# The weights' subtractions issued apart from their casts, and the next queries' split behind the softmax

## The chip, the cores and the metric

The kernel runs on one core of one Trainium2 chip. The metric is the device time of one execution in microseconds (us); the median of several runs is compared. The engines are TensorE (PE in the profile; its weight loads are PEld), VectorE (DVE), ScalarE (ACT), GpSimd (POOL) and SyncE (SP, which here issues the loads of the weights). Each engine works through its own queue in order; an instruction whose operands are not there yet holds up all that stand behind it.

## What is computed

The program is a model of two blocks on 512 rows of 1024 features, all in float32. The first block has two layers of token mixing (a pool branch, sparse attention over the best keys of an index, attention to a memory) followed by 16 experts of which each row uses two. The second block is a gated feed-forward stage, a mixer (a gated delta recurrence beside dilated band attention) and a second feed-forward stage. Cut to the parts that the change touches:

```python
def attend_block(args):                    # sparse attention, per 128 queries
    ...
    s = jnp.einsum('bqhd,bqkhd->bqhk', qb, kg) * (ATT_HEAD_DIM ** -0.5)
    p = jax.nn.softmax(jnp.where(valid[:, :, None, :], s, -jnp.inf), axis=-1)
    return jnp.einsum('bqhk,bqkhd->bqhd', p, vg)

def run_block(args):                       # one expert
    h = jax.nn.silu(xb @ w1[e]) * (xb @ w3[e])
    return h @ w2[e]

def second_block(x, ...):
    x = x + 0.5 * swiglu(rms_norm(x, ffn1_norm), ...)
    proj = rms_norm(x, mix_norm) @ w_in
    o_a = gdn_mixer(...)                   # recurrence
    o_b = dilated_mixer(...)               # band attention
    x = x + jnp.concatenate([o_a, o_b], axis=-1) @ w_out
    ...
```

## The kernel before

**Split products.** PE multiplies in a reduced float32 form. To keep float32 accuracy, both operands are split into a high half (a cast on ACT) and a low half (the original less the cast, on DVE), and each product is made of three: high by high, low by high, high by low. Names end in H and L: xTH, xTL are activations, wH, wL are weights, gH/gL and hH/hL the gathered rows and the hidden rows of an expert, qs the queries of an attention (one tile holds both halves).

**The stream of weights.** `Stream` cuts all weights into 708 units of up to 128 x 1024 and handles them in the order of use: `load` issues a transfer on SP into a staging buffer (wR, or one that is lent: wX, wY, wZ, X), `split` casts (line 182, wH<-wR) and subtracts (line 185, wL<-wR,wH) and then calls `load` for the next unit, since the staging buffer is free. 13 units are marked slow; their subtraction goes to POOL. `split` is called by `tick`, at most once in 1000 ns of the planner's time, as long as a place for the halves is free, or by `need`, when a product asks for a unit that has not been split. `Panel.H` and `Panel.L` hand the halves to the products.

**The planner.** The program is written out by a Python planner that keeps a clock of its own, `now`: each product adds an estimate of its time (`adv`, which also calls `tick`), and side tasks (attention, pooling, the recurrence) are generators that yield how long they want to wait. So the order of each engine's queue is fixed when the program is built.

**The attentions.** `paired` hands out scores for two heads at a time: `pair` makes both on PE (line 810, into two buffers sa), `scores` returns them one after the other. Before the second head's scores are returned, the next pair's queries are split (`halves`, which calls `split` of lines 355 and 356: a cast on ACT and a subtraction on DVE, 128 x 128). `attention` runs three stages over the heads: `first` takes the scores and makes the softmax (line 926 adds the mask and reduces on DVE, 928 is the exponential on ACT, 929 and 930 the reciprocal and the scaling on DVE), `second` transposes P on PE (line 890) and copies it out on ACT (892, PT), `third` multiplies with V (lines 294 and 303). Sparse attention (`dsa`) and band attention (`band_attention`) both use them.

**Other names in the rows.** pd/pdL and brL are splits of the pool branch; th are the products of an expert's hidden rows (lines 1352, 1353); cu is the convolution of the recurrence (1923), Gc its summed gates (2028), go and cs its output; mg and sig the gates that merge the branches.

Of the kernel before, what the change touches and what calls it, by code (L numbers as in the profile page):

```python
# [83 lines left out]
class Panel:  # L84
    def __init__(self, ws, key, units, n):
        self.ws, self.key, self.units, self.n = ws, key, units, n
        self.k = [(u, j) for u in units for j in range(u.kc)]
# [7 lines left out]
    def L(self, k):  # L95
        u, j = self.k[k]
        if u.L is None:
            self.ws.need(u)
        return u.L[:, j * u.n:(j + 1) * u.n]


class XT:


    def __init__(self, H, L):
        self.H, self.L, self.want = H, L, {}
# [15 lines left out]
class Stream:  # L122


    def __init__(self, kern, pool, nr, nh):
        self.kern, self.pool, self.nr, self.nh = kern, pool, nr, nh
        self.places = list(range(nh))
        self.units, self.panels = [], []
        self.issued = self.split_n = self.used = self.got = 0
        self.after, self.pace = 0.0, 1000  # L130
        self.base, self.lent = 0, []
        self.limit = 1 << 30

    def plan(self, key, w, kc, n, slow=False):
        per = max(1, 1024 // n)
        units = []
        k = 0
        while k < kc:
            m = min(per, kc - k)
            src = w[k * 128:(k + m) * 128, :].rearrange("(k p) n -> p k n", p=128)  # L140
            units.append(Unit(src, m, n))
            units[-1].slow = slow
            k += m
        self.units += units
        self.panels.append(Panel(self, key, units, n))
# [27 lines left out]
    def split(self):  # L173

        if self.split_n >= self.issued or self.split_n - self.used >= self.nh:
            return False
        nc = self.kern.nc
        u = self.units[self.split_n]
        n = u.kc * u.n
        u.H, u.L = self.turn([128, 1024], F32R, "w")  # L180
        eng = nc.vector
        nc.scalar.copy(u.H[:, :n], u.R[:, :n])  # L182
        if u.slow:
            eng = nc.gpsimd
        eng.tensor_tensor(u.L[:, :n], u.R[:, :n], u.H[:, :n].bitcast(F32), OP.subtract)  # L185
        self.split_n += 1
        if u.place is None:
            self.base -= 1
        else:
            self.lent.append(u.place)  # L190
        self.load()
        return True

    def turn(self, shape, dtype, name):

# [14 lines left out]

    def tick(self):

        if self.kern.now >= self.after and self.split_n < self.limit and self.split():
            self.after = self.kern.now + self.pace

# [17 lines left out]
class Kern:  # L233
# [581 lines left out]
    def paired(self, n, q, k, *pool):  # L815

        state = []

        def split(i):
            return self.halves(q(i), *pool) if i < n else None  # L820
        nxt = [0, split(0)]

        def scores():
            if not state:
                state.extend(self.pair(nxt[1], *k(nxt[0])))
                return state[0]
            nxt[:] = [nxt[0] + 1, split(nxt[0] + 1)]
            ps = state[1]
            state.clear()
            return ps  # L830
        return scores
# [45 lines left out]
    def attention(self, pool, scores, v, add, width, out, tag="sa"):  # L877
# [3 lines left out]
        nc = self.nc  # L881

        def first(st, qb, h):
            st["P"] = self.softmax(scores(), add(qb, h), width(qb), pool)

        def second(st, qb, h):
            W = width(qb)
# [192 lines left out]
    def ending(self, l, p, r, gb, last):  # L1080
# [23 lines left out]
        begin(0)  # L1104
        begin(1)
        split()
        scale(0)
        roots(0, 1)
# [1295 lines left out]
```

## Time and profile before

| | |
|---|---|
| median of 3 runs | 3045.59 us (3044.25 to 3047.68) |
| the profiled execution: its time, its span | 3044.89 us, 3043.2 us |
| mean granted clock of PE | 0.952 |
| PE busy | 2806.0 us, 92% |
| DVE busy | 1901.8 us, 62% |
| ACT busy | 1284.3 us, 42% |
| POOL busy | 445.7 us, 15% |

The span runs in stages, in us from its start: the first layer's mixing to 560 (sparse attention in 212 to 440) and its experts to 905, the second layer likewise to 1420 and 1795, the first feed-forward stage to 2180, the panels of the recurrence and the windows to 2385, band attention with the recurrence's chain to 2610, the output projection to 2650, the second feed-forward stage to the end. The busy shares are means over these stages. "Idle before, releaser" in a row says how long the engine stood just before an instruction and what ended that.

### The profile page before, as it was taken

What the parts mean: (1) busy time and instruction counts of PE and PEld (TensorE: products, weight loads), DVE (VectorE), ACT (ScalarE), POOL (GpSimd) and SP (SyncE); (2) the same over time, 40 slices, a digit from 0 to 9 for tenths busy, and PEclk for the clock granted to TensorE, in tenths of its full rate; (3) what the DMA queues carried; (4) which work ended last, traced back from release to release, by engine and by line L of the source; (5) the groups of instructions that cost most, each with busy time, mean ns of one, the idle gap of its engine ahead of it and who ended that gap; (6) DMA issues with size and microseconds to landing.
All of it is one profiled execution on the core that took longest, in us unless ns stands there. A gap on an engine that the chain in (4) does not pass through costs nothing. (4 is left out here: it accounts for less than half of the span.)

```text
span 3043.2 us, 38735 instructions
## 1 busy us (share of the span) xinstructions
PE 2806.0 (92%) x14315; PEld 2240.3 (74%) x14315; DVE 1901.8 (62%) x3535; ACT 1284.3 (42%) x2073; POOL 445.7 (15%) x526
## 2 busy tenths in 40 slices
PE   7989889999989898988899979999999697899998
PEld 7767668876757676777667757888888586688877
DVE  5677544798986776436799974333468636544244
ACT  3533432377863433422578832222345333322122
POOL 1000011264220000111552110000132121000000
PEclk9999999999989999999899979999999789899999
DMA  6212225899963122228799914323324400223231
GB/s 197 87 56 81 65 67 177 306 356 353 350 235 107 52 70 66 77 83 300 252 353 349 344 58 166 105 71 117 103 84 119 126 13 21 70 90 116 78 104 70
DMA packets 295587, 448.27 MB, mean 147 GB/s; under 512 B 30403, under 2 KB 155987, under 8 KB 294881
## 3 DMA queue, kind: packets, MB, share of 16 engines
q1 hardware_dynamic: 274816, 382.66, 38.3%
q0 software_dynamic: 20000, 60.99, 6.3%
q8 instruction: 114, 1.87, 0.3%
q10 hardware_dynamic: 576, 2.10, 0.2%
q14 instruction: 81, 0.66, 0.1%
HBM read 423.02 MB, written 34.65 MB: 150 GB/s over the span
## 5 line engine op out<-in xcount | busy, mean ns | idle before, releaser
L185 DVE TENSOR_TENSOR wL<-wR,wH 128x1024 fp32r<-128x1024 f32 (+2 forms) x381 | 469.2, 1254 | 269.3 <-ACT wH L182 260.2
L294 PE MATMUL mm<-xTH,wH 128*128 128x512 f32 (+1 forms) x1376 | 540.1, 393 | 0.1
L294 PE MATMUL mm<-xTH,wL 128*128 128x512 f32 (+1 forms) x1376 | 531.6, 386 | 7.5 <-DVE wL L185 7.5
L294 PE MATMUL mm<-xTL,wH 128*128 128x512 f32 (+1 forms) x1376 | 529.8, 385 | 2.3 <-DVE xTL L356 2.2
L182 ACT CAST wH<-wR 128x1024 fp32r<-128x1024 f32 (+1 forms) x394 | 399.6, 1041 | 255.1 <-PE mm L294 219.2
L294 PEld LDWEIGHTS mm<-xTH,wL 128*128 128x128 f32 x1376 | 263.2, 191 | 65.6 <-DVE wL L185 15.0
L294 PEld LDWEIGHTS mm<-xTH,wH 128*128 128x128 f32 x1376 | 264.3, 192 | 60.0 <-issue 8.9
L294 PEld LDWEIGHTS mm<-xTL,wH 128*128 128x128 f32 x1376 | 264.0, 192 | 49.8 <-DVE xTL L356 3.1
L294 PE MATMUL mm<-wH,hH 128*128 128x512 f32 (+1 forms) x608 | 241.0, 396 | 0.0
L294 PE MATMUL mm<-wH,hL 128*128 128x512 f32 (+1 forms) x608 | 239.2, 393 | 0.6 <-DVE hL L356 0.6
L294 PE MATMUL mm<-wL,hH 128*128 128x512 f32 (+1 forms) x608 | 238.6, 392 | 0.0
L294 PE MATMUL mm<-wH,xTH 128*128 128x256 f32 (+3 forms) x576 | 201.9, 351 | 10.8 <-DVE rx L758 5.3
L294 PE MATMUL mm<-wH,gH 128*96 128x512 f32 x512 | 206.7, 404 | 0.0
L294 PE MATMUL mm<-wH,gL 128*96 128x512 f32 x512 | 204.3, 399 | 0.0
L294 PE MATMUL mm<-wL,gH 128*96 128x512 f32 x512 | 203.0, 396 | 0.0
L294 PE MATMUL mm<-wH,xTL 128*128 128x256 f32 (+3 forms) x576 | 189.7, 329 | 3.6 <-DVE xTL L356 3.6
L294 PE MATMUL mm<-wL,xTH 128*128 128x256 f32 (+3 forms) x576 | 188.9, 328 | 0.0
L185 DVE TENSOR_TENSOR wL<-wX,wH 128x1024 fp32r<-128x1024 f32 x142 | 169.3, 1223 | 8.1 <-ACT wH L182 7.7
L182 ACT CAST wH<-wX 128x1024 fp32r<-128x1024 f32 x142 | 145.3, 1049 | 10.4 <-PE mm L294 9.6
L1664 DVE TENSOR_TENSOR th<-th,mm 128x512 f32<-128x512 f32 x44 | 30.3, 688 | 169.0 <-PE mm L294 169.0
L294 PEld LDWEIGHTS mm<-wH,hL 128*128 128x128 f32 (+1 forms) x608 | 107.3, 177 | 34.1 <-DVE hL L356 1.4
L294 PEld LDWEIGHTS mm<-wL,hH 128*128 128x128 f32 (+1 forms) x608 | 107.6, 177 | 30.5
(541 smaller groups left out, 5219.3 us busy)
## 6 DMA issues: line engine op xcount, KB each, us to landing
wX<-in_w SPq DMA_DIRECT2D x141, 512.0 KB, 11.3
wR<-in_w_in SPq DMA_DIRECT2D x116, 512.0 KB, 3.7
wR<-in_w SPq DMA_DIRECT2D x73, 512.0 KB, 11.0
wY<-in_w SPq DMA_DIRECT2D x69, 512.0 KB, 10.7
X<-in_w SPq DMA_DIRECT2D x56, 512.0 KB, 11.2
wZ<-in_w SPq DMA_DIRECT2D x45, 512.0 KB, 10.8
wR<-in_ffn_w_gate SPq DMA_DIRECT2D x44, 512.0 KB, 3.9
wR<-in_ffn_w_up SPq DMA_DIRECT2D x44, 512.0 KB, 4.7
```

What stands on the lines that cost most here:

```text
L182: nc.scalar.copy(u.H[:, :n], u.R[:, :n])
L185: eng.tensor_tensor(u.L[:, :n], u.R[:, :n], u.H[:, :n].bitcast(F32), OP.subtract)
L294: self.nc.tensor.matmul(ps, a, b, start=start, stop=stop)
L1664: nc.vector.tensor_tensor(th, th, u, OP.mult)
```

## The change

`split` no longer subtracts. It casts the unit, remembers it as `half`, and notes the planner's time; `subtract` issues the subtraction, gives the staging buffer back and calls `load`. `subtract` is called for a half unit by the next `split`, by `tick` once 1500 ns of the planner's time have passed since the cast, by `Panel.L` when a product asks for that unit's low half, and at once for a slow unit. In the attentions, the split of the next pair's queries moves from the place before the second head's scores are returned to the place behind that head's softmax. The first split of each attention stays where it was.

```diff
--- before.py
+++ after.py
@@ -96,6 +96,8 @@
         u, j = self.k[k]
         if u.L is None:
             self.ws.need(u)
+        if u is self.ws.half:
+            self.ws.subtract()
         return u.L[:, j * u.n:(j + 1) * u.n]
 
 
@@ -130,6 +132,7 @@
         self.after, self.pace = 0.0, 1000
         self.base, self.lent = 0, []
         self.limit = 1 << 30
+        self.half = None
 
     def plan(self, key, w, kc, n, slow=False):
         per = max(1, 1024 // n)
@@ -174,22 +177,30 @@
 
         if self.split_n >= self.issued or self.split_n - self.used >= self.nh:
             return False
-        nc = self.kern.nc
-        u = self.units[self.split_n]
+        if self.half:
+            self.subtract()
+        u = self.half = self.units[self.split_n]
         n = u.kc * u.n
         u.H, u.L = self.turn([128, 1024], F32R, "w")
-        eng = nc.vector
-        nc.scalar.copy(u.H[:, :n], u.R[:, :n])
+        self.kern.nc.scalar.copy(u.H[:, :n], u.R[:, :n])
+        self.split_n += 1
+        self.begun = self.kern.now
         if u.slow:
-            eng = nc.gpsimd
+            self.subtract()
+        return True
+
+    def subtract(self):
+
+        nc = self.kern.nc
+        u, self.half = self.half, None
+        n = u.kc * u.n
+        eng = nc.gpsimd if u.slow else nc.vector
         eng.tensor_tensor(u.L[:, :n], u.R[:, :n], u.H[:, :n].bitcast(F32), OP.subtract)
-        self.split_n += 1
         if u.place is None:
             self.base -= 1
         else:
             self.lent.append(u.place)
         self.load()
-        return True
 
     def turn(self, shape, dtype, name):
 
@@ -210,6 +221,9 @@
 
     def tick(self):
 
+
+        if self.half and self.kern.now >= self.begun + 1500:
+            self.subtract()
         if self.kern.now >= self.after and self.split_n < self.limit and self.split():
             self.after = self.kern.now + self.pace
 
@@ -820,11 +834,14 @@
             return self.halves(q(i), *pool) if i < n else None
         nxt = [0, split(0)]
 
-        def scores():
+        def scores(then=False):
+            if then:
+                if not state:
+                    nxt[:] = [nxt[0] + 1, split(nxt[0] + 1)]
+                return None
             if not state:
                 state.extend(self.pair(nxt[1], *k(nxt[0])))
                 return state[0]
-            nxt[:] = [nxt[0] + 1, split(nxt[0] + 1)]
             ps = state[1]
             state.clear()
             return ps
@@ -882,6 +899,7 @@
 
         def first(st, qb, h):
             st["P"] = self.softmax(scores(), add(qb, h), width(qb), pool)
+            scores(True)
 
         def second(st, qb, h):
             W = width(qb)
```

PE's and POOL's queues keep their order. Of the 695 weight subtractions on DVE, 264 stand later by 1 to 62 other instructions, mostly 1 to 6, and none earlier. Three places on DVE follow; lines 185, 356, 926, 929, 930, 1352, 1353, 1923 and 2028 of before are lines 198, 370, 944, 947, 948, 1370, 1371, 1941 and 2046 of the changed file.

DVE in the sparse attention of the first layer, at the second softmax of a pair over 384 keys (338 us in the trace). Before:

```order
L356 TENSOR_TENSOR pdL<-pd,pdH 128x512
L185 TENSOR_TENSOR wL<-wR,wH 128x1024
L356 TENSOR_TENSOR qs<-qT_1123,qs 128x128
L926 ISA P,st<-sa,sc 128x384
L926 ISA st 128x1
L929 RECIPROCAL st<-st 128x1
L930 TENSOR_SCALAR P<-P,st 128x384
L185 TENSOR_TENSOR wL<-wR,wH 128x1024
```

After:

```order
L370 TENSOR_TENSOR pdL<-pd,pdH 128x512
L944 ISA P,st<-sa,sc 128x384
L944 ISA st 128x1
L947 RECIPROCAL st<-st 128x1
L948 TENSOR_SCALAR P<-P,st 128x384
L370 TENSOR_TENSOR qs<-qT_1123,qs 128x128
L198 TENSOR_TENSOR wL<-wR,wH 128x1024 x2
L944 ISA P,st<-sa,sc 128x384
```

The P group moved ahead of one wL and of qs; both wL now stand behind it.

DVE at the experts of the first layer, one expert (the first rows are at 759 to 767 us in the trace, the last at 774; wX, wY, wR and X are staging buffers of the stream). Before:

```order
L185 TENSOR_TENSOR wL<-wY,wH 128x1024 x2
L356 TENSOR_TENSOR gL<-tp,gH 128x384 x2
L185 TENSOR_TENSOR wL<-wY,wH 128x1024 x2
L185 TENSOR_TENSOR wL<-X,wH 128x1024
L185 TENSOR_TENSOR wL<-wR,wH 128x1024
L1352 SCALAR_TENSOR_TENSOR th<-th,mm 96x512
L1353 TENSOR_TENSOR th<-th,mm 96x512
L185 TENSOR_TENSOR wL<-wR,wH 128x1024
L185 TENSOR_TENSOR wL<-X,wH 128x1024
L185 TENSOR_TENSOR wL<-wR,wH 128x1024
L356 TENSOR_TENSOR hL<-tp,hH 128x384
```

After:

```order
L198 TENSOR_TENSOR wL<-wY,wH 128x1024
L370 TENSOR_TENSOR gL<-tp,gH 128x384 x2
L198 TENSOR_TENSOR wL<-wY,wH 128x1024 x3
L198 TENSOR_TENSOR wL<-X,wH 128x1024
L1370 SCALAR_TENSOR_TENSOR th<-th,mm 96x512
L1371 TENSOR_TENSOR th<-th,mm 96x512
L198 TENSOR_TENSOR wL<-wR,wH 128x1024
L198 TENSOR_TENSOR wL<-X,wH 128x1024
L198 TENSOR_TENSOR wL<-wR,wH 128x1024
L370 TENSOR_TENSOR hL<-tp,hH 128x384
```

One wL moved behind the two gL, another behind the two th.

DVE in the recurrence's panels, ahead of the summed gates (2220 us in the trace). Before:

```order
L185 TENSOR_TENSOR wL<-wR,wH 128x1024
L1923 SCALAR_TENSOR_TENSOR cu<-cu,cw 128x512 x2
L185 TENSOR_TENSOR wL<-wR,wH 128x1024
L2028 COPY Gc<-sa 128x16
L2030 TENSOR_TENSOR nbg<-eG,gsm 128x16
L2031 TENSOR_SCALAR hb<-gsm 128x16
```

After:

```order
L1941 SCALAR_TENSOR_TENSOR cu<-cu,cw 128x512 x2
L198 TENSOR_TENSOR wL<-wR,wH 128x1024
L2046 COPY Gc<-sa 128x16
L2048 TENSOR_TENSOR nbg<-eG,gsm 128x16
L2049 TENSOR_SCALAR hb<-gsm 128x16
L2046 COPY Gc<-sa 128x16
L2048 TENSOR_TENSOR nbg<-eG,gsm 128x16
```

The first wL moved behind two products of cu, the second from ahead of Gc to a place further back.

## Rows read from the trace of the kernel before

**Rows 1.** PE's waits over the whole span: waiting line, awaited line, us, times, longest.

```profile
PE tp L890 <- DVE P L930: 31.4, 12, 5.3
PE tp L303 <- ACT PT L892: 25.4, 7, 9.3
...
PE mm L294 <- DVE wL L185: 8.3, 19, 0.5
```

**Rows 2.** Costliest groups of the page: busy us, mean ns, then idle before, releaser.

```profile
L185 DVE TENSOR_TENSOR wL<-wR,wH 128x1024 fp32r<-128x1024 f32 (+2 forms) x381 | 469.2, 1254 | 269.3 <-ACT wH L182 260.2
```

**Rows 3.** Timeline of DVE, 330 to 346 us: start, duration, instruction, idle before.

```profile
338.85 1.23 DVE L185 TENSOR_TENSOR wL<-wR,wH 128x1024 fp32r<-128x1024 f32 x1 [0.25 <-ACT wH L182]
...
340.19 0.55 DVE L926 CUSTOM_DVE_ANT_0 P<-sa,sc 128x384 f32<-128x384 f32 x1
```

**Rows 4.** Timelines of PE at three transposes of P, both layers.

```profile
342.29 0.88 PE L890 MATMUL tp<-ident,P 128*128 128x128 f32 x3 [4.24 <-DVE P L930]
...
427.71 1.09 PE L890 MATMUL tp<-ident,P 128*128 128x128 f32 x4 [5.31 <-DVE P L930]
...
1214.71 0.87 PE L890 MATMUL tp<-ident,P 128*128 128x128 f32 x3 [4.23 <-DVE P L930]
```

**Rows 5.** Timelines of DVE and POOL, 400 to 440 us.

```profile
422.85 2.34 DVE L185 TENSOR_TENSOR wL<-wR,wH 128x1024 fp32r<-128x1024 f32 x1
...
425.31 0.68 DVE L926 CUSTOM_DVE_ANT_0 P<-sa,sc 128x512 f32<-128x512 f32 x1
...
422.84 1.26 POOL L1063 TENSOR_TENSOR mg<-mg,sig 128x512 f32<-128x512 f32 x1 [0.62 <-DVE sig L1057]
```

**Rows 6.** Stretches: busy us of PE, PEld, DVE, ACT, POOL; granted clock; DMA.

```profile
340.11:346.94 6.83, 4.65 (x15) 3.43 (x16) 3.60 (x10) 3.42 (x7) 0.00 (x0) 0.50 0.55 153
...
600.00:880.00 280.00, 277.85 (x1341) 198.17 (x1339) 260.10 (x301) 222.69 (x275) 103.24 (x82) 0.99 1.03 353
2385.00:2610.00 225.00, 174.64 (x1318) 148.25 (x1316) 128.62 (x370) 77.73 (x210) 42.77 (x50) 0.83 0.20 55
```

**Rows 7.** DVE's waits from 2385 to 2610 us.

```profile
DVE qs L356 <- ACT qs L355: 18.2, 9, 3.2
```

**Rows 8.** Timelines of DVE, ACT and PE at one pair of band attention.

```profile
2584.87 0.29 DVE L356 TENSOR_TENSOR qs<-sqT,qs 128x128 fp32r<-128x128 f32 x1 [3.24 <-ACT qs L355]
...
2586.85 0.49 DVE L930 TENSOR_SCALAR P<-P,st 128x512 f32<-128x512 f32 x1
...
2584.54 0.30 ACT L355 CAST qs<-sqT 128x128 fp32r<-128x128 f32 x1
2585.80 0.72 ACT L928 ACTIVATE P<-P,st 128x512 f32<-128x512 f32 x1 [0.97 <-DVE st L926]
...
2586.44 0.79 PE L810 MATMUL sa<-skH,qs 64*128 64x512 f32 x2
```

**Rows 9.** Timelines of DVE and POOL, 2422 to 2428 us.

```profile
2424.42 2.63 DVE L930 TENSOR_SCALAR P<-P,st 128x512 f32<-128x512 f32 x1
...
2424.69 1.06 POOL L2197 TENSOR_TENSOR T<-C,blk 128x512 f32<-128x512 f32 x1
```

**Rows 10.** Timelines of DVE and PE at the summed gates.

```profile
2222.66 1.22 DVE L185 TENSOR_TENSOR wL<-wR,wH 128x1024 fp32r<-128x1024 f32 x1
...
2224.64 0.40 PE L2037 MATMUL sa<-ident,Gc 128*32 128x128 f32 x1 [6.04 <-DVE Gc L2028]
```

**Rows 11.** Timelines of DVE and PE at one expert of the first layer.

```profile
763.67 1.02 DVE L356 TENSOR_TENSOR gL<-tp,gH 128x384 fp32r<-128x384 f32 x2
765.00 2.36 DVE L185 TENSOR_TENSOR wL<-wY,wH 128x1024 fp32r<-128x1024 f32 x2 [0.31 <-ACT wH L182]
...
768.41 1.22 DVE L185 TENSOR_TENSOR wL<-wR,wH 128x1024 fp32r<-128x1024 f32 x1
769.55 0.68 DVE L1352 SCALAR_TENSOR_TENSOR th<-th,mm 96x512 f32<-96x512 f32 x1
...
771.87 0.39 PE L294 MATMUL mm<-wL,hH 128*96 128x512 f32 x1
```

## The prediction

> **What bounds the kernel now.** I read the page first. TensorE (PE) is by far the busiest engine (the table above), so a change on VectorE (DVE) or ScalarE (ACT) gains only where PE stands and waits for them. The waits of PE over the whole span say where that is. The largest sum is the transposes of softmax rows that wait for the scaled P on DVE (31.4 us, 12 times); next come the products with V that wait for ACT's copy of the transposed P (25.4 us, 7 times). The weights' low halves wL, which the change moves most, cost PE only 8.3 us in 19 waits of at most 0.5 us [rows 1]. So the stream's subtractions are no bottleneck as such. What they do is stand in DVE's queue: 381 of the largest form take 469.2 us busy, and another 269.3 us of DVE's idle time lies in front of them, 260.2 us of it put down to the cast on ACT [rows 2]. While DVE waits for a cast, nothing behind it starts. Where a softmax that PE waits for is what stands behind, that is on the path. The same holds for the next queries' subtraction qs, which waits for its own cast.
>
> The profiled run took 3044.9 us, 1.7 us more than its span; the median of the three runs is 3045.6. I make the sum against 3044.9 and add 0.7 at the end.
>
> **Part 1, sparse attention (both layers of the first block).** The second softmax of each pair has the next queries' split in front of it. At 338 us DVE had a wL, the qs, then the score reduction into P (line 926); afterwards the P group comes first, then qs and wL (the first place of the order, above). The reduction itself needs only scores that PE has long delivered at the two places below.
>
> First place: DVE is free 0.25 us ahead of the wL at 338.85, so at 338.6, and the reduction started at 340.19 [rows 3]. Without wL and qs ahead of it, it can start 1.6 us sooner. ACT does not give that back, since its cast of qs moves behind the exponential too. PE stood 4.24 us for this P [rows 4]; what is late next is the same P, 1.6 us earlier. Second place: the wL took 2.34 us, from 422.85, and the reduction started at 425.31, 2.46 us after it could have [rows 5], out of a stall of 5.31 us [rows 4]. The qs comes just behind P now, but ahead of the next pair's scores PE still has the four transposes of that P, 1.09 us [rows 4], so the pair does not wait for it. Two smaller stalls of this kind, at 318 and 302 us, lose a wL and a qs in front of their P, but at the first the wL then stands before a split of the pool branch (brL) that PE waits for next; I count 0.9 us for both, less than the 1.23 of one wL [rows 3]. Sum 1.6 + 2.46 + 0.9 = 4.96 a layer, and layer 2 has the same stalls 871 us later, the first of them 4.23 us long [rows 4]: **9.9 us**. Bounds: 8.1 (the two large ones alone) and 11.
>
> **Part 2, the clock.** [...] Taken **4 us** (1 a dip), bounds 0 and 9.3.
>
> **Part 3, band attention (2385 to 2610 us).** PE is busy 174.64 of 225 us there [rows 6]; DVE and ACT pass work to each other. DVE waited for the cast of qs 9 times, 18.2 us together [rows 7]. At 2584.87 one sees what that cost: DVE stood 3.24 us while ACT worked off its queue, the cast ran from 2584.54, the exponential at 2585.80 only, and P's scaling at 2586.85 [rows 8]. With the reduction done ahead, in those 3.24 us, the exponential takes the cast's place at 2584.54: 1.26 us sooner. The pair's scores start at 2586.44 and need qs [rows 8]; P would be scaled from 2585.6 to 2586.1, and qs behind it ends at 2586.3. I count five such places (2399, 2417, 2501, 2563 and 2585 us): 5 x 1.26 = **6.3 us**; at the other four something else ends about as late. Bounds: 0 (the chain there runs through POOL and the recurrence too) and 9 (half of the 18.2).
>
> [...] One P of this stretch took 2.63 us for a scaling of 0.49, while POOL ran tensor operations from 2424.69 on [rows 9, 8]; the wL of 2.34 us likewise ran beside a POOL product of 1.26 us [rows 5], against 1.23 elsewhere [rows 3]. [...]
>
> **Part 4, the recurrence's panels (2180 to 2385 us).** PE stood 6.04 us for Gc until 2224.64. In front of Gc DVE had two wL; the one of 2222.66, 1.22 us long, now stands behind it [rows 10], so I take 1.2 us. A second large stall there, at 2365 us, waits for a chain that starts with a transfer of what DVE wrote before: between 0 and 1.2, and I take 0.5, since nothing shows whether that transfer or the chain decides. **1.7 us**, bounds 0 and 3.
>
> **Part 5, what may be lost: the experts.** From 600 to 880 us PE is busy 277.85 of 280 us and DVE 260.10 [rows 6], so there is nothing to gain. But subtractions now stand behind gL, hL and the products of th. I replayed one expert by hand. The wL that ran ahead of the two gL, while these waited for their cast, now runs behind them, from 764.65; the next, before at 765.00, are 0.8 us late; the one of 768.41 goes behind the two th (769.55 and after it, 0.68 us each) and ends at 771.81 instead of 769.63, while PE uses it at 771.87 [rows 11]. That holds by 0.06 us; the others hold by 0.4 us or more, and DVE has 1.2 us to spare in a period of 17.7 us (260.10 of 280 busy) to make the lag up. I take a cost of **1 us** in all, bounds 0 and 16 (1 us for each of the 16 experts of this layer; the weights of the second layer's experts are ready earlier). In the two feed-forward stages the subtraction that PE waits for stays where it is. The loads follow the subtractions by at most 2.3 us, and PE's waits name no weight load [rows 1]: nothing. In the mixers' projections as many wL stand ahead of what PE waits for as before, others in number only: nothing.
>
> Sum: 9.9 + 4 + 6.3 + 1.7 - 1 = 20.9, so 3044.9 - 20.9 = 3024.0, and with 0.7 for the median 3024.7: **3025 us**.
>
> **The rivals.** A: only the sparse attention gains. For it: the band stretch is a tangle of chains, and a wait taken away there often gives way to another that ends within a few tenths. Then 9.9 + 2 of the clock - 1 = 10.9: 3045.6 - 10.9, about 3035. B: most is given back, because the displaced qs and wL are waited for elsewhere, above all by the next pair's scores (0.1 us of margin at 2586). 1 us at each of the 15 later pairs of band attention takes 15 of the 20.9: 3045.6 - 5.9, about 3040, on the edge of no change. C, slower: the margin of 0.06 us at the experts does not hold. It decides from the point where the lag passes the use at 771.87 by more than the 1.2 us of spare time make up before the next expert; from there DVE sets the period in the first layer. At 2.2 us of lag (771.81 - 769.63) for each of 16 experts it costs 35 us: 3024.7 + 35, about 3060. Against it: in the replay the lag is made up within each period, and PE hardly waits for wL today. D: the change does not do what it says, because the planner's clock issues most subtractions at once after all. The order rules that out: 264 of the 695 subtractions on DVE stand later, mostly by 1 to 6 instructions; so D has no chance of its own.
>
> **How the numbers follow.** Chances: forecast 0.60, A 0.16, B 0.14, C 0.10. With all upper bounds, 11 + 9.3 + 9 + 3 = 32.3, the time is 3013; chains that I did not follow may add a little, so the range starts at 3009. Above, it takes in A and nearly all of B and leaves out C: 3044. About 0.2% (6 us) is what a measurement of this kernel can tell from no change, so faster means below 3039.5. The forecast lies there but for a tail of 0.02, A but for 0.02, and B with a small part, 0.03: 0.75 faster; 0.15 within; 0.10 slower.
>
> **What would show it.** In the profile after: PE's wait for P down from 31.4 to about 22 us, its stalls at 338 and 422 us at 2.6 and 2.9 us; no qs in front of the reductions any more; the half-clock stretches there shorter. The experts are right if their stretch keeps its length within 1 us and no PE wait for wL appears in it. The forecast is wrong if the pair's scores (line 810) wait for qs, or if wL becomes a wait of PE well above its 8.3 us.

## The result

The changed kernel takes 3005.25 us, the median of 4 runs (2999.22 to 3007.87), against 3044.92 us (3039.83 to 3047.68) for the kernel before in the same comparison: a ratio of 0.9873, interval 0.9862 to 0.9885. The direction was right and the size was not: 39.7 us came where the prediction's sum had 20.9, and 3005 lies below the range, which ended at 3009.

The profiled execution after took 3007.87 us, its span is 3006.2 us, 37.0 less than before, and the mean granted clock of PE is 0.960 (0.952 before). The first line of the page after (engine, busy us, share of the span, instructions):

```profile
PE 2792.3 (93%) x14315; PEld 2227.8 (74%) x14315; DVE 1885.5 (63%) x3535; ACT 1283.9 (43%) x2073; POOL 447.3 (15%) x526
```

PE issues the same 14315 products in the same order in both kernels, so that each product of the one has its partner in the other. PE's busy time fell from 2806.0 to 2792.3, so 13.7 of the 37.0 us are the same products done faster. The granted clock is enough for them, by an estimate: of PE's busy time, 203.3 us lay in stretches at half clock before and 170.9 after. In the trace of before, products of 128 x 512 start 0.43 us apart at half clock (345.37 to 346.23 us) and 0.23 us apart at the full one (from 347.02 on), so about half of that difference, 16.2 us, is what the clock took. The other 23.3 us are idle time of PE. This split is one of the time and not of its causes: slower products can fill a wait that was idle otherwise, as in the middle of the band, where PE was busy 9.4 us less at a clock of 1.00 than at 0.83 and 3.6 of these became idle time (experiment 8). One profiled run below, that of experiment 9, took 3044.26 us, where the other four of its kernel took 2999 to 3007, and lost 38 us at the start of band attention; only its stages ahead of that are read. Between the same pairs of products, by stage (starts in the trace of before; "half clock" is the time in which the granted clock was 0.50; both traces show this value and 1.00 and no other):

| stage, us of before | length before, after | change | of it idle | of it busy | half clock before, after |
|---|---|---|---|---|---|
| mixers' projections, 120 and 1001 | 176.5, 180.1 | +3.6 | +3.0 | +0.6 | 13.7, 13.7 |
| first queries, 212 and 1085 | 177.9, 173.1 | -4.8 | -1.7 | -3.1 | 6.8, 0 |
| sparse attention, 302 to 440 | 138.0, 130.1 | -7.9 | -5.0 | -3.0 | 23.9, 13.7 |
| sparse attention, 1173 to 1310 | 137.2, 127.8 | -9.5 | -5.7 | -3.8 | 28.1, 15.1 |
| panels, 2181 to 2385 | 203.9, 197.2 | -6.7 | -4.6 | -2.1 | 23.9, 13.7 |
| band attention, 2385 to 2650 | 265.2, 258.6 | -6.6 | -6.4 | -0.2 | 81.9, 81.9 |
| all else | | -5.1 | -3.0 | -2.1 | |

Windows of the kernel after over the four lower stages say the same (busy us of PE, PEld, DVE, ACT, POOL, then PE's granted clock, DMA share, GB/s):

```profile
302.00:432.10 130.10, 117.50 (x611) 89.18 (x610) 67.37 (x165) 55.41 (x113) 12.02 (x8) 0.95 0.24 69
1162.40:1290.10 127.70, 115.84 (x591) 87.76 (x589) 67.25 (x163) 53.69 (x110) 12.03 (x8) 0.94 0.24 70
2157.30:2354.50 197.20, 178.79 (x1186) 163.67 (x1188) 144.51 (x327) 89.21 (x159) 47.27 (x152) 0.97 0.39 107
2354.50:2613.10 258.60, 213.30 (x1483) 180.72 (x1480) 139.22 (x393) 85.60 (x219) 46.26 (x51) 0.84 0.20 58
```

and those of before over the same work:

```profile
302.10:440.10 138.00, 120.45 (x611) 91.41 (x610) 71.40 (x164) 55.63 (x112) 12.16 (x8) 0.91 0.22 65
1173.10:1310.30 137.20, 119.67 (x592) 90.51 (x590) 71.26 (x163) 54.36 (x109) 12.15 (x8) 0.90 0.22 66
2181.20:2385.00 203.80, 180.80 (x1186) 165.28 (x1188) 143.64 (x326) 88.80 (x159) 49.90 (x152) 0.94 0.36 101
```

PE's waits over the span of the kernel after (waiting line, awaited line, us, times, longest), which answer [rows 1]:

```profile
PE tp L908 <- DVE P L948: 22.0, 12, 2.7
PE tp L317 <- ACT PT L910: 21.7, 7, 8.0
...
PE tp L979 <- DVE kL L800: 10.9, 2, 5.4
...
PE mm L308 <- DVE wL L198: 8.8, 20, 0.5
```

The wait for P went from 31.4 to 22.0 us, as forecast, and wL stayed where it was (8.3, 8.8). New is the length of the third line's wait: kL cost 7.9 us, 4.4 at most, before. DVE's own largest group of subtractions, which answers [rows 2], stands 170.9 us idle ahead of itself instead of 269.3:

```profile
L198 DVE TENSOR_TENSOR wL<-wR,wH 128x1024 fp32r<-128x1024 f32 (+2 forms) x381 | 463.6, 1236 | 170.9 <-ACT wH L185 169.9
```

**The two large stalls of sparse attention.** DVE and PE of the kernel after at the first (timeline: start, duration, instruction, idle before), to hold against [rows 3, 4]:

```profile
334.53 0.69 DVE L370 TENSOR_TENSOR pdL<-pd,pdH 128x512 fp32r<-128x512 f32 x1 [0.74 <-ACT pdH L369]
335.14 0.55 DVE L944 CUSTOM_DVE_ANT_0 P<-sa,sc 128x384 f32<-128x384 f32 x1
336.67 0.42 DVE L948 TENSOR_SCALAR P<-P,st 128x384 f32<-128x384 f32 x1
337.00 0.29 DVE L370 TENSOR_TENSOR qs<-qT,qs 128x128 fp32r<-128x128 f32 x1
337.21 2.35 DVE L198 TENSOR_TENSOR wL<-wR,wH 128x1024 fp32r<-128x1024 f32 x2
```

```profile
337.24 0.52 PE L908 MATMUL tp<-ident,P 128*128 128x128 f32 x3 [2.53 <-DVE P L948]
...
418.99 1.09 PE L908 MATMUL tp<-ident,P 128*128 128x128 f32 x4 [2.69 <-DVE P L948]
```

The reduction into P follows the pool branch's pdL at once; qs and two wL come behind the scaling. The stalls are 2.53 and 2.69 us; 2.6 and 2.9 were forecast. The two lines on PE also differ in what no forecast had: three transposes in 0.52 us are at the full clock (1.00 from 337.24 to 341.00 us; they took 0.88 in [rows 4]), four in 1.09 at half (0.66 in the mean from 418.99 to 428.00), as before.

**Band attention.** DVE's wait for the cast of qs, 18.2 us in 9 times before [rows 7], is one of 7.4 us, in the wait list of DVE from 2354 to 2580 us; that one stands ahead of the first pair, whose split the change leaves in its place:

```profile
DVE st L947 <- ACT P L946: 31.6, 32, 3.1
...
DVE qs L370 <- ACT qs L369: 7.4, 1, 7.4
```

The pair of [rows 8] after the change, ACT, DVE and PE:

```profile
2550.89 0.72 ACT L946 ACTIVATE P<-P,st 128x512 f32<-128x512 f32 x1
...
2551.61 0.29 ACT L369 CAST qs<-sqT 128x128 fp32r<-128x128 f32 x1
2551.93 0.49 DVE L948 TENSOR_SCALAR P<-P,st 128x512 f32<-128x512 f32 x1
2552.33 0.28 DVE L370 TENSOR_TENSOR qs<-sqT,qs 128x128 fp32r<-128x128 f32 x1
2553.47 0.79 PE L824 MATMUL sa<-skH,qs 64*128 64x512 f32 x2
```

The exponential took the cast's place, qs ends at 2552.61, and the pair's scores start at 2553.47, behind the transposes: 0.86 us of margin.

**The summed gates and the experts.** DVE ahead of Gc, and PE that waits for it, against [rows 10]; then one expert against [rows 11]:

```profile
2195.53 1.54 DVE L1941 SCALAR_TENSOR_TENSOR cu<-cu,cw 128x512 f32<-128x512 f32 x2 [3.22 <-ACT cu L1936]
2197.08 1.22 DVE L198 TENSOR_TENSOR wL<-wR,wH 128x1024 fp32r<-128x1024 f32 x1
2198.22 0.17 DVE L2046 COPY Gc<-sa 128x16 f32<-128x16 f32 x1
...
2199.06 0.28 PE L2055 MATMUL sa<-ident,Gc 128*32 128x128 f32 x1 [3.45 <-DVE Gc L2046]
```

```profile
759.62 0.69 DVE L1371 TENSOR_TENSOR th<-th,mm 96x512 f32<-96x512 f32 x1
760.23 1.22 DVE L198 TENSOR_TENSOR wL<-wR,wH 128x1024 fp32r<-128x1024 f32 x1
...
761.56 0.41 PE L308 MATMUL mm<-wL,hH 128*96 128x512 f32 x1
```

The stall for Gc fell from 6.04 to 3.45. The expert's wL ends at 761.45 and PE uses it at 761.56: 0.11 us of margin, 0.06 in the replay by hand. The stage of the first experts (600 to 905 us) became 0.4 us shorter.

### The profile page after: what moved, and what is told of

Its sections match the earlier page's. It is cut to its first block, busy times and chain, and to the rows that moved or that the text cites. A ratio compares the mean times of both kernels' runs of the same rounds, so it can differ in the third digit from the quotient of the medians.

```text
span 3006.2 us, 38642 instructions
## 1 busy us (share of the span) xinstructions
PE 2792.3 (93%) x14315; PEld 2227.8 (74%) x14315; DVE 1885.5 (63%) x3535; ACT 1283.9 (43%) x2073; POOL 447.3 (15%) x526
## 5 line engine op out<-in xcount | busy, mean ns | idle before, releaser
L198 DVE TENSOR_TENSOR wL<-wR,wH 128x1024 fp32r<-128x1024 f32 (+2 forms) x381 | 463.6, 1236 | 170.9 <-ACT wH L185 169.9
L308 PEld LDWEIGHTS mm<-xTH,wL 128*128 128x128 f32 x1376 | 260.9, 190 | 65.5 <-DVE wL L198 15.1
L308 PEld LDWEIGHTS mm<-wH,hH 128*128 128x128 f32 (+1 forms) x608 | 107.5, 177 | 30.0
## 6 DMA issues: line engine op xcount, KB each, us to landing
wR<-in_w SPq DMA_DIRECT2D x73, 512.0 KB, 10.9
wZ<-in_w SPq DMA_DIRECT2D x45, 512.0 KB, 10.9
```

The source lines that it names most:

```text
L308: self.nc.tensor.matmul(ps, a, b, start=start, stop=stop)
```

## The experiments

Three questions were open: which half of the change brings what, what the clock brings by itself, and where the unforeseen gains and losses come from. The theory was that P, Gc and the exponential were delayed by what stood ahead of them in DVE's and ACT's queues, and that PE's clock follows PE's stalls. The rival was that the half-clock stretches go their own way and that the surplus is chance. Stage changes below are against the kernel before, between the same products of PE; the line numbers in an experiment's rows are those of its own kernel.

**1 and 2. Each half alone.** First the queries' split moved, with the subtraction issued with its cast as before; then the subtractions apart, with the queries' split in its old place.

```diff
 (queries alone, in split)
-        if u.slow:
-            self.subtract()
+        self.subtract()
         return True
 (subtractions alone, in scores and first)
+            nxt[:] = [nxt[0] + 1, split(nxt[0] + 1)]
             ps = state[1]
...
             st["P"] = self.softmax(scores(), add(qb, h), width(qb), pool)
-            scores(True)
```

> The changed kernel with each weight subtracted right behind its cast again; only the next queries' split stays behind the softmax. Theory (the subtractions in front of the softmaxes and Gc carry the change in the sparse attention and the panels; the queries carry it in band attention): band attention about 6 us shorter (2385 to 2650 of before), the sparse attention only 1 to 2 us a layer, the panels and the experts as before; in all 8 to 10 us less than before, about 3036. Rival (the queries' split in front of the second softmax is what holds the sparse attention too): 20 us or more less, 3025 or below, with the stall of 4.24 us at 338 down to about 2.5.

> The changed kernel with the next queries' split back in front of the second softmax; only the subtractions stand apart from their casts. Theory: the sparse attention keeps 8 to 10 of its 10 to 12 us a layer, the panels keep their 7, the mixers' 4 us loss stays, band attention gives its 6 us back; 25 to 29 us less than before, about 3018. Rival (the queries carry the sparse attention): 15 us less at most, 3030 or above. If the two parts help only together (the softmax has to lose both of what stands in front of it, since the queries' cast is waited for anyway), e1 and e2 add up to much less than the 37 to 40 us of the whole change.

Measured: queries alone 3036.11 us, ratio 0.9984 (0.9961 to 1.0007); subtractions alone 3020.37, 0.9933 (0.9906 to 0.9960). The ratios add up to a gain of 0.8%, and both together give 1.27%; by the medians it is 33.0 us and 39.7. With intervals this wide the totals leave open how much is missing (the two profiled runs gained 11.8 and 26.6 us, which would leave nothing). The sparse attention shows it stall by stall. At 338 us PE's stall for P is, with the queries alone and then with the subtractions alone:

```profile
343.69 0.87 PE L907 MATMUL tp<-ident,P 128*128 128x128 f32 x3 [4.01 <-DVE P L947]
```

```profile
337.60 0.87 PE L904 MATMUL tp<-ident,P 128*128 128x128 f32 x3 [3.65 <-DVE P L944]
```

against 4.24 before and 2.53 with both. At 422 us it is 5.11 with the queries alone and 4.17 with the subtractions alone, against 5.31 before and 2.69 with both. So one half alone gives 0.2 or 0.6 us of 1.7 at the first place and 0.2 or 1.1 of 2.6 at the second, since DVE then still waits for the other's cast and works it off. DVE with the subtractions alone:

```profile
335.29 0.29 DVE L370 TENSOR_TENSOR qs<-qT,qs 128x128 fp32r<-128x128 f32 x1 [0.83 <-ACT qs L369]
335.50 0.55 DVE L940 CUSTOM_DVE_ANT_0 P<-sa,sc 128x384 f32<-128x384 f32 x1
```

PE's idle time in the sparse attention of the first layer fell by 0.7 (queries), 1.9 (subtractions) and 5.0 us (both). The panels and the first queries' stages are the work of the subtractions alone: -6.6 and -4.9 us with them, -0.1 and +0.1 without. In the band the idle time fell by 2.0, 1.1 and 6.4 us, and the length by 10.3, 5.1 and 6.6, the queries alone gaining most; experiment 8 shows how little such numbers of the band can bear.

**3. The subtractions apart in the sparse attentions only**, together with the queries' split; everywhere else each subtraction is issued with its cast.

```diff
-        if u.slow:
+        if u.slow or not any(lo <= self.split_n <= hi for lo, hi in ((44, 64), (312, 332))):
             self.subtract()
```

> The changed kernel in which subtractions stand apart from their casts only for the units that are cast while the sparse attentions run (some 20 of each layer); all others follow their cast at once; the queries' split is moved everywhere. Theory (the gain of the subtractions is mainly in the sparse attention): about 22 us from the sparse attentions and 6 from band attention, 3017, and the mixers' loss of 1.7 and 1.9 us is gone. Rival (the order elsewhere, in the panels, the routing and the experts, carries half): 3028 or above.

Measured: 3027.76 us, 0.9951 (0.9930 to 0.9972), about what the rival said. The two sparse attentions are 17.9 us shorter than before, as much as with the whole change (17.4); what this kernel lacks lies elsewhere. The panels are 1.5 us longer than before, where the whole change made them 6.7 shorter, so their gain hangs on the subtractions there. And this kernel shows the clock apart from the stalls. Its two layers have the same large stalls (2.53 and 2.68 us in the first, 2.55 and 2.68 in the second), and the windows over them are:

```profile
301.50:434.80 133.30, 121.12 (x612) 92.03 (x611) 68.09 (x165) 55.61 (x113) 12.02 (x8) 0.91 0.23 68
1166.10:1290.30 124.20, 110.67 (x591) 84.07 (x590) 66.93 (x163) 53.66 (x111) 12.01 (x8) 0.99 0.25 72
```

The idle times (length less PE's busy time) are 12.2 and 13.5 us. But the first layer ran at a mean clock of 0.91 and gained 4.9 us, the second at 0.99 and gained 13.0.

**4 and 5. The clock by itself.** Products whose results are overwritten, put into the stalls ahead of the transposes of P, so that PE works while it waits: in the kernel before (4, 4, 12, 16 and 6 of them at five heads of each layer) and in the kernel after (3, 7, 8 and 6 at four).

```diff
             pt = self.psum("tp")
+            for _ in range(FILL.get((qb, h), 0) if fill is not None else 0):
+                nc.tensor.matmul(pt, fill[:, 0, 0:128], fill[:, 0, :], start=True, stop=True)
             for j in range(W // 128):
```

> The kernel before, with idle-time products on PE added: 4 to 16 products of 128 x 512 into the buffer of the transposes, ahead of the transposes of five heads a layer at which PE waits for P (1.96, 1.74, 4.24, 5.31 and 2.25 us in the trace); the transposes overwrite them. Nothing else moves. Theory (a good part of what the change gave in the sparse attention came from the granted clock, which falls to 0.50 after these stalls): the half-clock stretches there (24 us in layer 1, 28 in layer 2) mostly vanish, PE's stalls keep their ends, and the time falls by 6 to 12 us to about 3036. Rival (PE's work at half clock lies under DVE's and ACT's chain and costs nothing): within 2 us of before, or slower by what the added products cost.

> The changed kernel, with 3 to 8 idle products of 128 x 512 on PE ahead of the transposes of four heads a layer at which PE still waits for P (1.17, 2.53, 2.69 and 2.25 us in the trace after). Theory (the clock is a price of its own beside the stalls, and the change took about half of the half-clock time of the sparse attentions): the other half, 13.7 and 15.1 us in the profiled run, mostly goes, worth 5 to 8 us: about 2998. Rival (what is left at half clock there lies under DVE's chain): 3003 to 3007 as the changed kernel.

Measured: before with the idle products 3026.9 us, 0.9944 (0.9929 to 0.9959), a larger gain than the theory's 6 to 12 us; after with them 3001.26, 0.9855 (0.9837 to 0.9873). In the kernel before, no instruction of the other engines is moved or made shorter: P comes sooner only as far as PE's own work ahead of it does. PE at 338 us, then the windows of both layers:

```profile
335.51 2.93 PE L891 MATMUL tp<-kH 128*128 128x512 f32 x12
339.82 0.55 PE L893 MATMUL tp<-ident,P 128*128 128x128 f32 x3 [1.38 <-DVE P L933]
```

```profile
302.40:433.30 130.90, 122.18 (x653) 93.12 (x652) 71.19 (x164) 55.33 (x112) 12.19 (x8) 1.00 0.23 69
1165.90:1295.70 129.80, 121.44 (x636) 92.69 (x634) 71.44 (x163) 54.44 (x111) 12.20 (x8) 0.99 0.24 69
```

The stages became 7.1 and 7.8 us shorter and hold 42 products more, at a clock of 1.00 and 0.99 instead of 0.91 and 0.90: 14.9 us in the two sparse attentions of before were the price of the clock alone, more than the 9.3 that the prediction set as its upper bound. The median fell by 17.8 us, so this is not the chance of one profile. In the kernel after, the same means took the two layers to -9.7 and -13.6 us; the median is 4.0 us below the plain changed kernel's, between the theory and its rival, with intervals that overlap.

**6. The mixers' loss.** The subtractions of the units cast in the mixers' projections issued with their casts.

```diff
-        if u.slow:
+        if u.slow or any(lo <= self.split_n <= hi for lo, hi in ((24, 31), (294, 301))):
             self.subtract()
```

> The changed kernel in which the 8 units a layer that are cast during the mixers' projections just ahead of the sparse attention are subtracted at once, as before. Theory (setting these subtractions back made the memory attention's stall at 188 us a microsecond longer and cost 1.7 and 1.9 us): 2 to 4 us less than the changed kernel, with that stall back at 4.4 us; 3002. Rival (the loss there is a shift of the clock by chance): no change of the stall, within 1 us.

Measured: 3004.99 us, 0.9873 (0.9854 to 0.9892). The two stages are back at their old lengths (-0.1 and 0.0 us), and PE's wait for kL too:

```profile
PE tp L979 <- DVE kL L800: 7.9, 2, 4.4
```

DVE shows why kL was late: between the rotation of the rows and kL one wL stood before, and in the changed kernel there are two, the second put off into the middle of a search for the best keys, behind which kL comes. The kernel before, then the changed one:

```profile
186.57 1.22 DVE L185 TENSOR_TENSOR wL<-wR,wH 128x1024 fp32r<-128x1024 f32 x1
...
191.98 0.41 DVE L786 TENSOR_TENSOR kL<-tp,kH 128x256 fp32r<-128x256 f32 x1
```

```profile
187.19 1.22 DVE L198 TENSOR_TENSOR wL<-wR,wH 128x1024 fp32r<-128x1024 f32 x1
...
191.29 1.22 DVE L198 TENSOR_TENSOR wL<-wR,wH 128x1024 fp32r<-128x1024 f32 x1
...
193.62 0.41 DVE L800 TENSOR_TENSOR kL<-tp,kH 128x256 fp32r<-128x256 f32 x1
```

The cause of the longer wait is shown; the 2 to 4 us that the theory promised of the whole did not show in the medians (3004.99 against 3005.25), which cannot tell so little apart.

**7. How long to put off.** No wait on the planner's clock: a subtraction is issued at the next tick behind its cast.

```diff
-        if self.half and self.kern.now >= self.begun + 1500:
+        if self.half and self.kern.now >= self.begun:
```

> The changed kernel with the subtraction handed out at the next call of the planner's tick, whatever its clock says, instead of 1500 ns after the cast. Theory (what helps is that the subtraction stands behind the few instructions that the same step issues, as the P group at 338 and 422 us): most of the gain stays, 3005 to 3012. Rival (the time of 1500 ns matters, since a tick comes with every product and the subtraction would be back in front of the softmax): the gain falls to that of the queries' split alone, about 3036.

Measured: 3023.57 us, 0.9938 (0.9917 to 0.9958), about half of the gain, so neither the theory nor its rival. At 338 and 422 us the stalls are 2.55 and 2.68 us, as with the whole change, so one tick is enough there. The smaller stall that ended at 320 us, 1.74 us before and 0.06 with the whole change, is 1.53; the panels (-0.3 us, the idle time -0.1) and the first queries (no change of the idle time in either layer) lose what they had. It is these that need the 1500 ns.

**8. Is the clock's gain steady?** The changed kernel with eight idle products at about 118 us, which shifts what follows by at most 2 us up to the band and changes none of it.

```diff
                 pt = self.psum("tp")
+                self.idle("mem", pt)      (8 products at its first call)
                 for t in range(2):
```

> The changed kernel with eight idle products of 128 x 128 (1.7 us of PE) ahead of the first transposes of the memory attention of layer 1, at about 118 us, and nothing else: all that follows runs 0 to 2 us later. Theory (which stretch runs at half clock after a given stall depends on when the stall falls): the stalls keep their lengths, single stretches of half clock in the sparse attentions and in band attention change by 3 to 7 us either way, and the whole stays within 6 us of the changed kernel. Rival (the stall's length alone sets the half-clock time): the same stretches to 0.5 us, and 0 to 2 us slower.

Measured: 3003.39 us, 0.9868 (0.9850 to 0.9885), within the changed kernel's interval. Behind the mixers its profiled stages agree with the changed kernel's within 0.7 us but in three: the last feed-forward stage is 1.6 us shorter, the first sparse attention 1.8, and the middle of the band is, in the changed kernel and then in the shifted one:

```profile
2465.20:2528.10 62.90, 54.19 (x377) 46.66 (x377) 35.27 (x106) 17.89 (x41) 16.31 (x16) 0.83 0.08 25
```

```profile
2464.70:2521.80 57.10, 44.77 (x378) 38.33 (x377) 36.51 (x106) 17.64 (x41) 16.15 (x16) 1.00 0.08 28
```

The same work took 5.8 us less at a clock of 1.00 instead of 0.83: PE was busy 9.4 us less, and 3.6 of these became idle time. Over the whole of band attention, the kernel before and then the shifted one:

```profile
2385.00:2650.20 265.20, 213.50 (x1483) 180.10 (x1482) 142.82 (x393) 85.50 (x219) 45.17 (x51) 0.85 0.20 56
```

```profile
2353.77:2607.48 253.71, 201.03 (x1483) 170.41 (x1480) 141.78 (x393) 85.22 (x219) 46.02 (x51) 0.89 0.20 59
```

It is 11.5 us shorter than before and PE's idle time is 1.0 longer, where the changed kernel, with the same order in it, has 6.6 us less, nearly all of it idle time. And in experiment 4, which changes nothing in the band, the band came out 3.4 us shorter:

```profile
2371.20:2633.00 261.80, 212.78 (x1483) 179.93 (x1480) 140.85 (x393) 85.43 (x219) 46.39 (x51) 0.84 0.19 57
```

In the sparse attention the stall is the same 2.69 us, but the transposes behind it run at the full clock here, and at half in the changed kernel (1.09 us, above); here the granted clock fell only at 424.41, 6 us later (0.81 in the mean from 418.40 to 428.00):

```profile
418.40 0.63 PE L921 MATMUL tp<-ident,P 128*128 128x128 f32 x4 [2.69 <-DVE P L963]
```

So the theory came in the main, though in the band the waits changed too, and a stage's length in one profile holds up to some 6 us that no instruction of the stage accounts for. That it is the shift that decides is not shown: there is one profile of each kernel, and the four runs of the changed kernel alone span 2999 to 3008 us, with mean granted clocks of 0.959 to 0.965. For band attention, then, the rival named at the head of this section stands.

**9 to 11. Idle products further on.** To see whether the clock can be held elsewhere: idle products of 128 x 128 in 14 more stalls (memory attention, band, experts' ends, routing, panels, norm) on top of 5 and 6; then 5 and 6 alone; then these with only the ends of the experts, the routing, the norm, one mixer's projection and one convolution filled (8 to 20 products at each).

```diff
+    def idle(self, site, ps=None):
+        k = self.seen[site] = self.seen.get(site, -1) + 1
+        n = FILLS.get((site, k), 0)
+        if n:
+            ps = self.psum("tp") if ps is None else ps
+            for _ in range(n):
+                self.nc.tensor.matmul(ps[:, 0:128], self.ident, self.ident, start=True, stop=True)
```

> The kernel e6 with the idle products of e5 and with 7 to 24 more (128 x 128) at each of some 13 further stalls of PE over 2.5 us (memory attention, the ends of the experts, routing, the norm ahead of the first feed-forward stage, the recurrence's panels, band attention). Theory (half-clock time is paid wherever PE has work in it): 245 us at half clock fall to some 150 and the time by 15 to 30 us against the changed kernel, to about 2980. Rival (outside the sparse attention the half-clock stretches lie in thin work that the other engines bound): no more than e5 and e6 together, 2995.

> The kernel e6 with the idle products of e5 in the sparse attentions alone. Theory: the 3.4 us of the mixers in e6 and the 5 us of e5 add up, 2998. Rival: as e5, 3001, since what the mixers gain only shifts where the clock falls.

> The kernel e6 (mixers' subtractions at once) with the idle products of e5 in the sparse attentions and 8 to 20 of 128 x 128 at six stalls outside the attentions: the ends of both layers' experts, the routing of layer 2, the norm ahead of the first feed-forward stage, one convolution of the panels. None in the memory attention and in band attention, where e7 lost. Theory (clock and order add up): 2994, against 3005 of the changed kernel. Rival (the clock's falls move elsewhere as the stages shift in time, and the sum is no better than e5): 3001.

Measured: 3002.42 us, 0.9861 (0.9842 to 0.9881) for the widest; 3001.35, 0.9862 (0.9847 to 0.9877) for the sparse attentions alone; 2997.31, 0.9838 (0.9821 to 0.9856) for the last. The widest missed its theory's 2980 by far and its rival's 2995 too; the second came out as its rival said, the last between the two. The widest lost 3.6 and 2.9 us in the mixers' projections, which hold the memory attention, where PE was busy 4.8 and 2.8 us more; that its products delay what they stand ahead of is the likely reason, not a tested one. What it did in band attention is not known. The last is the fastest kernel of this study, and its interval lies just below the changed kernel's (0.9862 to 0.9885). Its sparse attentions are 12.0 and 11.6 us shorter than before, the first at the full clock throughout, with 24 products more:

```profile
299.20:425.40 126.20, 118.33 (x635) 89.87 (x634) 67.23 (x164) 54.98 (x113) 12.05 (x8) 1.00 0.24 71
```

## Why the prediction was wrong in size

Term by term, against the profiled 37.0 us (the median moved by 2.7 more, since the execution profiled after took 3007.87 us, above its median):

| term | forecast | measured |
|---|---|---|
| Part 1, stalls of sparse attention | 9.9 (8.1 to 11) | 12.4, of it 1.7 in the first queries' stages |
| Part 2, clock there | 4 (0 to 9.3) | 9.8, of it 3.1 in the first queries' stages |
| Part 3, band attention | 6.3 (0 to 9) | 6.6 |
| Part 4, panels | 1.7 (0 to 3) | 6.7 |
| Part 5 and all the rest | -1 | +1.5 (mixers -3.6, the rest +5.1) |

The 16.1 us between the sum and the profile come mainly from three places: the panels (5.0), the first queries' stages, which no term of the sum held (4.8), and the clock in the sparse attentions (2.7).

**Part 1 was right in mechanism and nearly in size.** 10.6 us lie in the two stages that it spoke of, with the stalls that it named. What failed is what it left out without a reason, the first queries: a wait of 1.43 us at 214 us fell to 0.56 there, in each layer, and a half-clock stretch of 3.4 us behind it went, 4.8 us in all. It also did not say that the halves need each other; experiments 1 and 2 show that either alone leaves most of the stall.

**Part 2 failed in its working: the clock was priced too low.** Its 4 us, 1 for each of four dips, and its bound of 9.3 are terms that no run shows. What the runs show: the two sparse attentions held 52.0 us at half clock, where the stretch at the first large stall is 6.83 us with 4.65 us of PE work in it [rows 6]; experiment 4 puts 14.9 us on the clock there. Nor did the fall come again where it had been. Before, the clock fell at 340.11 [rows 6] while PE stood, until 342.29 [rows 4]; with P 1.6 us sooner PE would have met that fall 0.6 us into it. After, at 337.24, there was no fall at all: the stall of 2.53 us passed at the full clock, while the one of 2.69 us at 416 did not. In the two stages that the term spoke of, the clock gave 6.7 us, within its bounds; 3.1 more came in the first queries' stages. The bounds should have come from the granted clock over the whole stage (0.91 and 0.90 there), not from the dips behind the stalls that were being shortened.

**Part 3 was near in its number by luck.** At 2584.87 of before all came as described: the exponential in the cast's place, qs behind the scaling, no wait of the pair's scores. PE's idle time fell by 6.4 us, 6.3 were forecast. But the forecast put that on the queries' split, and the queries alone took off 2.0; and with the same order in the band, the shifted kernel of experiment 8 lost no idle time at all. In the changed kernel PE ran at half clock for 21.3 us from 2500 to 2560 instead of 7.5, and its slower products filled waits: the two at 2511 and 2518 us of before, 1.49 and 2.30 us, are 0.35 and 0.86 there, but 1.50 and 2.42 in the shifted one. In the six profiles with this order (the changed kernel and experiments 5, 6, 8, 10 and 11) the band is 4.2 to 11.5 us shorter than before, and in experiment 4, with nothing changed in it, 3.4; what the split is worth there stays open. One scaling of 2.63 us beside POOL's work was there before [rows 9], and one is there after:

```profile
2390.55 2.63 DVE L948 TENSOR_SCALAR P<-P,st 128x512 f32<-128x512 f32 x1
...
2390.82 1.06 POOL L2215 TENSOR_TENSOR T<-C,blk 128x512 f32<-128x512 f32 x1
```

It moved with the rest and was not doubled: of the other 31 scalings there, none took more than 1.34 us before and 1.05 after.

**Part 4 is the step that failed most, by a factor of four.** It took the one wL that went from ahead of Gc, 1.2 us. The stall shrank by 2.6 (6.04 to 3.45), because the other wL mattered as well: it stood ahead of cu and waited for its cast, and DVE's idle time there fell from 4.77 us, in this line of the kernel before, to the 3.22 us that cu itself waits (above):

```profile
2220.07 1.23 DVE L185 TENSOR_TENSOR wL<-wR,wH 128x1024 fp32r<-128x1024 f32 x1 [4.77 <-ACT wH L182]
```

The prediction priced the moved instruction by its own duration and not by the wait that it brought along; it had said so itself of [rows 2], that a wL ahead holds up what is behind. Two more stalls followed: one of 1.5 us at 2302 is gone, and the large one for cu went from 8.43 to 7.2, the upper bound of 1.2 that the prediction allowed. The clock gave 2.1. Unlike the band's, this gain is steady: 6.6 to 6.8 us in the profiles of experiments 2, 6 and 8.

**Part 5 erred in sign, by 2.5 us.** The experts' margin held, and rival C did not come: 0.11 us instead of 0.06. "Nothing" for the mixers was wrong: the number of wL ahead of kL was not the same (one before, two after), 3.6 us. Against that, 5.1 us came in pieces of up to 2.2 at the ends of the experts, the routing and the stages behind it, 3.0 of them idle time; what delayed PE at each was not followed.

Of the rivals, none came. A and B have longer times than the forecast, the panels gained too, and the pair's scores did not wait for qs (0.86 us of margin at 2553). What the range lacked is a case with more gain than the forecast: the upper bounds of the terms were added up to 3013. In the stages that the terms spoke of only the panels' was exceeded (6.7 against 3); the first queries' 4.8 us and the 5.1 us of the rest stood in no term.

## What to carry to other kernels

A low-priority instruction ahead of a critical one in its queue cost its duration here and also the wait for its own operands (at Gc the stall shrank by 2.6 us, where 1.2 were priced): price both, and where two such stand there, move both, since moving one alone may bring little (here 0.2 or 0.6 us, and 1.7 with both). Putting work off helped where the critical instruction came first (PE's wait for P, 31.4 to 22.0 us) and hurt where it came next (its wait for kL, 7.9 to 10.9), so look at each place where PE waits. Price PE's clock over the whole stage from its granted clock, not stall by stall, and try idle products in the stalls that cannot be removed (14.9 us in experiment 4); a few us between two profiles of one stage (5.8 in the middle of the band) are no evidence of anything until a second profile, as of a kernel shifted in time, shows them again.

## What was not expected of the hardware

Two stages that held stalls of up to 4 to 5 us lost nearly half as much again to the clock: 14.9 us beside 35 us of idle time, given back by 84 idle products and nothing else. Of two equal stalls of 2.69 us, in the same place of two kernels that stand 0.6 us apart there, one saw the clock fall to half before PE went on (at 418.28) and the other 6 us after it; the middle of the band, likewise, took 62.9 us in the one and 57.1 in the other. Band attention, in which PE waits for others, even showed less idle time where its clock was lower: 45.3 us at a mean clock of 0.84 and 52.7 at 0.89, in these two. And the runs of the kernel before, 26 in the comparison of experiments 1 to 4, spread from 3030 to 3051 us, their mean granted clocks from 0.950 to 0.959; what sets the clock's falls in one run and not in the next was not found.
